# Turning the merged activations to channel-major with VectorE block transposes and DMAs through DRAM instead of TensorE transposes

## The chip, the cores and the metric

The kernel runs on one core of one Trainium2 chip. The metric is the device time of an execution in microseconds; a kernel's time is the median of its runs. A core has five engines with instruction streams of their own: TensorE (PE, matrix products), VectorE (DVE), ScalarE (ACT), GpSimd (POOL) and SyncE (SP, which here only issues DMAs). Each engine works through its stream in order, and engines wait for each other by semaphores.

## The reference

One layer of a decoder trunk on 256 tokens of 2048 channels. After an RMSNorm, one wide projection feeds three branches (stick-breaking attention, a Mamba-2 scan, cross-attention into 256 memory tokens) and three sets of gates. What matters here is the end:

```python
gates = sigmoid(gate_pre + b_gate)
g_sb, g_ssd, g_mem = split(gates, 3)
merged = (g_sb * (o_sb @ w_branch_sb)
          + g_ssd * (o_ssd @ w_branch_ssd)
          + g_mem * (o_mem @ w_branch_mem))
x = x + merged @ w_out
return rms_norm(x, final_norm_w)
```

All is float32. The kernel keeps the precision by splitting each operand of a product into a high and a low part and adding three products.

## The kernel before, in words

**Layout.** `merged` is held token-major: two tiles of 128 tokens x 2048 channels. The last product contracts over channels, so its left operand must be channel-major: `mT`, a `Cols` object of sixteen blocks of 128 channels (four to a slot), each with a high and a low half of 128 x 256 tokens. Turning `merged` into `mT` is the subject of the change.

**A gemm.** `gemm` (L249) computes 256 tokens x 512 output channels. It goes over the contraction in chunks of two 128-row blocks. For each chunk `load_chunk` (L205) issues a DMA of 512 KB of weights on SP's queue into a `raw` buffer (four of them, `RAWB`). `split` (L142) lets ScalarE write the high part `wh` (L146) and VectorE the low part `wl` (L150), each with three buffers. Then come twelve matmuls (L266 to L268): for each of two blocks and two token halves high x high, high x low, low x high. A gemm over 2048 rows has 16 blocks, eight chunks.

**The order of work.** The code is emitted by hand in program order and each engine keeps that order. After each chunk `pump` (L185) advances a counter, runs what has fallen due, and takes one step of other work from one of two lanes. `defer(fn, chunks)` (L172) puts `fn` on a heap, due so many chunks later. `gemm` defers its evacuation by `LATE` = 3 chunks, so it is emitted in the middle of the next gemm, behind that gemm's third chunk on every queue.

**The stage of the change.** The loop at L866 takes the branches in the order memory, stick-breaking, scan, and for each four groups `g` of 512 channels: a gate gemm (hidden state times gate weights, evacuated with bias and sigmoid into `sig`) and a branch gemm, whose `branch_evac` (L850) multiplies by the gate on VectorE (L857) and adds into `merged` on GpSimd (L858). For the third branch (`br == 2`), a group of `merged` is then complete. One chunk later `merged_cols` (L834) is emitted twice: TensorE turns eight 128x128 blocks into PSUM (L838), and two chunks after that `split` writes their high and low parts into `mT`. For `g` = 0 to 2 this falls into the gate gemm of the next group; for `g` = 3 into the first of the four output gemms. These read `mT` block by block, so that in their first gemm chunk 6 (blocks 12, 13) and chunk 7 (blocks 14, 15) need the last group.

**The output.** Three output gemms (L932) use `gemm`; the fourth (L936 on) splits its weights into slots first and computes the token halves one after the other, so that the first half is normalised and written while the second is computed.

The tiles of `slot` (L66) come from one pool of 16 buffers of 8 KB per partition.

Of the kernel before, what the change touches and what calls it, by code (L numbers as in the profile page):

```python
# [10 lines left out]
F32 = mybir.dt.float32  # L11
# [5 lines left out]
P = 128  # L17
D = 2048
T = 256
NKT = D // P  # L20
GW = 512
# [4 lines left out]
LATE = 3  # L26
# [15 lines left out]
def trunk_kernel(  # L42
# [6 lines left out]
    nc = tc.nc  # L49
# [6 lines left out]
    dram = ctx.enter_context(tc.tile_pool(name="dram", bufs=1, space=bass.MemoryType.DRAM))  # L56
# [5 lines left out]
    def nm(s):  # L62
        cnt[0] += 1
        return f"{s}_{cnt[0]}"

    def slot(shape, dt=F32, n="slot"):  # L66
        return big.tile(shape, dt, tag="slot", name=nm(n))

    def t4(shape, n="t4"):
        return tmp.tile(shape, F32, tag="t4", name=nm(n), bufs=2)  # L70
# [16 lines left out]
    def bank(shape, n="bank"):  # L87
        return psB.tile(shape, F32, tag="bank", name=nm(n))
# [11 lines left out]
    ident = const.tile([P, P], F32, name="ident")  # L100
# [41 lines left out]
    def split(*parts):  # L142


        for hi, _, src, scale in parts:
            nc.scalar.activation(hi, src, AF.Copy, **({} if scale is None else {"scale": scale}))  # L146
        for hi, lo, src, scale in parts:
            h32 = hi.bitcast(F32)
            if scale is None:
                nc.vector.tensor_tensor(lo, src, h32, ALU.subtract)  # L150
            else:
                nc.vector.scalar_tensor_tensor(lo, src, scale, h32, ALU.mult, ALU.subtract)
# [19 lines left out]
    def defer(fn, chunks=LATE):  # L172

        cnt[0] += 1
        heapq.heappush(late, (now[0] + chunks, cnt[0], fn))
# [9 lines left out]
    def pump():  # L185


        now[0] += 1
        while late and late[0][0] <= now[0]:
            heapq.heappop(late)[2]()  # L190
        advance(lanes[now[0] % 2])

    def finish():
        while lanes[0] or lanes[1]:
            for lane in lanes:
                advance(lane)
# [8 lines left out]
    def load_chunk(w, c0, width, k0, kc):  # L205
        raw = stage.tile([P, kc, width], F32, tag="raw", name=nm("raw"), bufs=RAWB)
        nc.sync.dma_start(
            raw, w[k0 * P:(k0 + kc) * P, c0:c0 + width].rearrange("(k p) n -> p k n", p=P))
        return raw
# [36 lines left out]
            nc.scalar.activation(dst, acc[:, :, 1], AF.Copy)  # L246
            nc.vector.tensor_tensor(dst, acc[:, :, 0], dst, ALU.add)

    def gemm(lhs, nk, w, c0, evac):  # L249

        acc2 = psA.tile([P, 2, GW], F32, tag="acc", name=nm("acc"), bufs=2)
        acc = [acc2[:, 0], acc2[:, 1]]
        kc = KC
        for k0 in range(0, nk, kc):
            raw = load_chunk(w, c0, GW, k0, kc)
            wh = stage.tile([P, kc, GW], F32R, tag="wh", name=nm("wh"))
            wl = stage.tile([P, kc, GW], F32R, tag="wl", name=nm("wl"))
            split((wh, wl, raw, None))
            for j in range(kc):
                kt = k0 + j  # L260
                lh, ll = lhs.at(kt)
                first, last = kt == 0, kt == nk - 1
                for t in range(2):
                    a = acc[t]
                    tt = slice(t * P, (t + 1) * P)
                    nc.tensor.matmul(a, lh[:, tt], wh[:, j], start=first, stop=False)  # L266
                    nc.tensor.matmul(a, lh[:, tt], wl[:, j], start=False, stop=False)  # L267
                    nc.tensor.matmul(a, ll[:, tt], wh[:, j], start=False, stop=last)  # L268
            pump()
        defer(lambda: evac(acc))  # L270

    def to_cols(dst, b0):

# [165 lines left out]
    for g in range(4):  # L439
        gemm_cols(memT, NKT, w_mem_kv, 2 * g * P, to_split_cols(kT, 2 * g),  # L440
                  acc=None if g else [bank([P, 2, T], "acc") for _ in range(2)])
# [161 lines left out]
    for g in range(2):  # L603
        gemm(hT, NKT, w_in, C_SBV + g * GW, to_rows(vS, g * GW))
# [226 lines left out]
    merged = [slot([P, D], F32, "merged") for _ in range(2)]  # L831
    mT = []

    def merged_cols(k0):  # L834
        ps = bank([P, 2, T], "mt")
        for j in range(2):
            for t in range(2):
                nc.tensor.transpose(ps[:, j, t * P:(t + 1) * P],  # L838
                                    merged[t][:, (k0 + j) * P:(k0 + j + 1) * P], ident)
        defer(lambda: split((*mT[0].at(k0, 2), ps, None)), 2)  # L840

    def gate_evac(c0, sig):
        nc.scalar.dma_start(sig[:, 0], b_gate[c0:c0 + GW].partition_broadcast(P))
        def evac(acc):
            for t in (1, 0):
                nc.vector.tensor_tensor(sig[:, t], acc[t], sig[:, 0], ALU.add)
            defer(lambda: sigmoid(sig), 1)
        return evac

    def branch_evac(br, g, sig):  # L850
        cs = slice(g * GW, (g + 1) * GW)
        def evac(acc):
            for t in range(2):
                if br == 0:
                    nc.vector.tensor_tensor(merged[t][:, cs], acc[t], sig[:, t], ALU.mult)
                else:
                    nc.vector.tensor_tensor(sig[:, t], acc[t], sig[:, t], ALU.mult)  # L857
                    nc.gpsimd.tensor_tensor(merged[t][:, cs], merged[t][:, cs], sig[:, t],  # L858
                                            ALU.add)
            if br == 2:  # L860
                for pr in range(2):
                    defer(lambda pr=pr: merged_cols(4 * g + 2 * pr), 1)
        return evac

    branches = ((4096, oM, 8, w_branch_mem), (0, oS, 8, w_branch_sb), (2048, None, 16, w_branch_ssd))
    for br, (g0, src, nk, wb) in enumerate(branches):  # L866
        for g in range(4):
            sig = t4([P, 2, GW], "sig")
            gemm(hT, NKT, w_in, C_GATE + g0 + g * GW, gate_evac(g0 + g * GW, sig))
            if src is None:  # L870
                finish()
                mT.append(Cols(NKT, "mT"))
                src = oD[0]
            gemm(src, nk, wb, g * GW, branch_evac(br, g, sig))


    yo = [slot([P, D], F32, "yo") for _ in range(2)]
# [58 lines left out]
    g = 3  # L936
# [9 lines left out]
    for t in range(2):  # L946
        tt = slice(t * P, (t + 1) * P)
        for cs in (slice(0, GW),) if t == 0 else (slice(0, T), slice(T, GW)):
            acc = psA.tile([P, 2, GW], F32, tag="acc", name=nm("acc"),
                           bufs=2)[:, 0, 0:cs.stop - cs.start]  # L950
# [50 lines left out]
```

## Time and profile before

| what | value |
|---|---|
| median of 3 runs | 1228.02 us (1227.74 to 1228.5) |
| span of the profiled execution, first to last instruction | 1226.6 us |
| TensorE busy | 1215.5 us |
| VectorE / ScalarE / GpSimd busy | 784.2 / 649.1 / 51.2 us |
| read from HBM / written | 239.48 MB / 2.13 MB |
| mean granted TensorE clock | 0.998 |

The profile is of one execution. Of that execution the profile gives the span only; the runs' median lies 1.4 us above it, which is what surrounds the first and the last instruction. A row of a timeline reads: start in us, duration in us, engine, source line, operation, written tile `<-` read tiles, shape, count, and in brackets how long the engine was idle before it and what ended the idling. A suffix q (SPq, ACTq) marks a DMA issue on that engine's queue: its duration is that of issuing, not of moving the data. In the chain of work that ended last a row is start, duration and what the time went to. A row for a tile or a line gives durations in ns as minimum/median/maximum. A row of windows gives the stretch and its length, the busy time of PE, its weight loads, VectorE, ScalarE and GpSimd, the granted clock, the DMA share and GB/s. A row of DMA issues ends with the KB of each and the median us from issue to landing.

### The profile page before, as it was taken

The page shows a single profiled execution, that of the slowest core. Times are in us where ns is not written, and L with a number is a line of the kernel's source. Part 1 is how long each engine was busy: PE and PEld are TensorE (multiplying, and loading weights), DVE is VectorE, ACT ScalarE, POOL GpSimd, SP SyncE. Part 2 cuts the span into 40 slices and gives each one's busy share as a digit, 9 for nine tenths or more (in the row PEclk, how much of TensorE's full clock was granted, in tenths as well). Part 3 has the DMA queues.
Part 4 walks back from the last instruction along what each step waited for, and adds up shares of the span by engine and source line. Part 5 has one row for each costly group of instructions (what it writes and reads, how often), then busy time and mean ns, then how long its engine had stood idle before and what let it go on. Part 6 is the DMA issues. An engine that isn't in the chain of part 4 may idle for free.

```text
span 1226.6 us, 16569 instructions
## 1 busy us (share of the span) xinstructions
PE 1215.5 (99%) x6388; PEld 1034.8 (84%) x6388; DVE 784.2 (64%) x990; ACT 649.1 (53%) x875; POOL 51.2 (4%) x50
## 2 busy tenths in 40 slices
PE   9999999999999999999999999999999999999997
PEld 7888888888888888888888888888888888888886
DVE  5686554565654555888888758676777755555554
ACT  6765443554445454545665756475756544444443
POOL 0000000000000000010100000000000010110101
PEclk9999999999999999999999999999999999999999
DMA  9966566655566656565567667686766666567673
GB/s 340 342 197 187 163 194 189 187 168 165 166 180 182 187 172 182 169 182 173 177 185 223 207 200 218 180 231 181 231 184 192 202 195 205 188 197 240 204 240 107
DMA packets 175023, 242.70 MB, mean 198 GB/s; under 512 B 10272, under 2 KB 109792, under 8 KB 174816
## 3 DMA queue, kind: packets, MB, share of 16 engines
q1 hardware_dynamic: 168224, 229.51, 61.2%
q10 hardware_dynamic: 6720, 12.13, 3.0%
q8 instruction: 50, 0.82, 0.3%
q14 instruction: 29, 0.24, 0.1%
HBM read 239.48 MB, written 2.13 MB: 197 GB/s over the span
## 4 chain that ended last, share of the span: by engine, by line
PE 96%; DMA 1%; issue 1%; DVE 1%; ACT 1%; SPq 0%; POOLq 0%; POOL 0%; ACTq 0%
PE acc L229 29%; PE acc L266 15%; PE acc L267 15%; PE acc L268 15%; PE acc L233 14%; PE acc L398 1%; PE acc L399 1%; PE acc L397 1%; PE y L773 1%; DMA raw<-in_w_out_dram 1%; DMA raw<-in_w_mem_kv_dram 1%; PE dtp L459 0%; PE xp L730 0%; PE mt L838 0%; PE spo L649 0%
## 5 line engine op out<-in xcount | busy, mean ns | idle before, releaser
L150 DVE TENSOR_TENSOR wl<-raw,wh 128x1024 fp32r<-128x1024 f32 (+1 forms) x409 | 502.8, 1233 | 310.3 <-ACT wh L146 308.1
L146 ACT ACTIVATE wh<-raw 128x1024 fp32r<-128x1024 f32 (+1 forms) x409 | 431.0, 1055 | 382.5 <-PE acc L268 200.7
L229 PE MATMUL acc<-hT,wh 128*128 128x512 f32 x1408 | 444.0, 397 | 0.0
L233 PEld LDWEIGHTS acc<-hT,wl 128*128 128x128 f32 x1408 | 264.5, 188 | 62.5
L233 PE MATMUL acc<-hT,wl 128*128 128x256 f32 x1408 | 276.8, 278 | 0.0
L229 PEld LDWEIGHTS acc<-hT,wh 128*128 128x128 f32 x1408 | 214.4, 189 | 0.1
L266 PE MATMUL acc<-wh,hT 128*128 128x512 f32 x448 | 175.9, 393 | 0.0
L267 PE MATMUL acc<-wl,hT 128*128 128x512 f32 x448 | 174.7, 390 | 0.0
L268 PE MATMUL acc<-wh,hT 128*128 128x512 f32 x448 | 174.6, 390 | 0.0
L266 PEld LDWEIGHTS acc<-wh,hT 128*128 128x128 f32 x448 | 84.1, 188 | 17.7 <-ACT sq L146 0.5
L268 PEld LDWEIGHTS acc<-wh,hT 128*128 128x128 f32 x448 | 84.1, 188 | 17.8
L267 PEld LDWEIGHTS acc<-wl,hT 128*128 128x128 f32 x448 | 84.1, 188 | 17.4 <-DVE wl L150 0.6
L266 PE MATMUL acc<-wh,oD 128*128 128x512 f32 x128 | 49.8, 389 | 0.0
L267 PE MATMUL acc<-wl,oD 128*128 128x512 f32 x128 | 49.8, 389 | 0.0
L268 PE MATMUL acc<-wh,oD 128*128 128x512 f32 x128 | 49.8, 389 | 0.0
L687 DVE SCALAR_TENSOR_TENSOR cT<-cu,wcols,cT 128x255 f32<-128x255 f32 (+2 forms) x96 | 46.4, 483 | 3.4
L858 POOL TENSOR_TENSOR merged<-merged,sig 128x512 f32<-128x512 f32 x16 | 25.1, 1588 | 521.9 <-DVE sig L857 521.9
L229 PE MATMUL acc<-memT,wh 128*128 128x512 f32 x128 | 40.5, 398 | 0.0
L266 PE MATMUL acc<-wh,mT 128*128 128x512 f32 x96 | 37.4, 390 | 0.0
L268 PE MATMUL acc<-wh,mT 128*128 128x512 f32 x96 | 37.4, 389 | 0.0
L267 PE MATMUL acc<-wl,mT 128*128 128x512 f32 x96 | 37.4, 389 | 0.0
L630 POOL TENSOR_TENSOR lm<-lm,sp 128x384 f32<-128x384 f32 x8 | 13.1, 1639 | 394.7 <-DVE sp L629 385.0
(250 smaller groups left out, 1301.4 us busy)
## 6 DMA issues: line engine op xcount, KB each, us to landing
raw<-in_w_in_dram SPq DMA_DIRECT2D x288, 512.0 KB, 3.8
raw<-in_w_branch_ssd_dram SPq DMA_DIRECT2D x32, 512.0 KB, 4.1
raw<-in_w_out_dram SPq DMA_DIRECT2D x32, 512.0 KB, 5.1
raw<-in_w_mem_kv_dram SPq DMA_DIRECT2D x31, 512.0 KB, 6.6
raw<-in_w_branch_mem_dram SPq DMA_DIRECT2D x16, 512.0 KB, 4.1
raw<-in_w_branch_sb_dram SPq DMA_DIRECT2D x16, 512.0 KB, 4.5
dec<-acT SPq DMA_DIRECT2D x24, 256.0 KB, 6.2
sig<-in_b_gate_dram ACTq DMA_DIRECT2D x12, 256.0 KB, 4.7
```

What stands on the lines that cost most here:

```text
L146: nc.scalar.activation(hi, src, AF.Copy, **({} if scale is None else {"scale": scale}))
L150: nc.vector.tensor_tensor(lo, src, h32, ALU.subtract)
L229: nc.tensor.matmul(halves[b], wh[:, kt - k0, b * P:(b + 1) * P], lhs.both(kt), start=first, stop=False, skip_group_check=True)
L233: nc.tensor.matmul(halves[b][:, 1], wl[:, kt - k0, b * P:(b + 1) * P], lhs.at(kt)[0], start=False, stop=last, skip_group_check=True)
L266: nc.tensor.matmul(a, lh[:, tt], wh[:, j], start=first, stop=False)
L267: nc.tensor.matmul(a, lh[:, tt], wl[:, j], start=False, stop=False)
L268: nc.tensor.matmul(a, ll[:, tt], wh[:, j], start=False, stop=last)
L397: nc.tensor.matmul(a, lh[:, tt], wh[:, g], start=first, stop=False)
L398: nc.tensor.matmul(a, lh[:, tt], wl[:, g], start=False, stop=False)
L630: nc.gpsimd.tensor_tensor(lm, lm, sp, ALU.subtract)
L687: nc.vector.scalar_tensor_tensor(a[:, s:T], u[:, 0:T - s], convw[:, 3 - s, i:i + 1], a[:, s:T], ALU.mult, ALU.add)
L858: nc.gpsimd.tensor_tensor(merged[t][:, cs], merged[t][:, cs], sig[:, t], ALU.add)
```

## The change

`merged_cols` and its TensorE transposes go. A new function `turn` takes their place. For a group, VectorE transposes the 32x32 blocks of 128 tokens x 512 channels within the partitions, once for each token half; one DMA on SP's queue writes the result (512 KB) to a DRAM tile `turned`; two chunks later four DMAs on SP's queue read it back, each to 32 partitions and in pieces of 512 B, so that a channel's 256 tokens come to lie in one partition. Then four `split`s of one block each write `mT`, two of them two chunks after the reads and two of them three chunks after. `gemm` gets an argument for its evacuation's delay; it is 1 instead of 3 for the last group of the third branch. `turn` uses a further slot per group.

```diff
-    def gemm(lhs, nk, w, c0, evac):
+    def gemm(lhs, nk, w, c0, evac, chunks=LATE):
...
-        defer(lambda: evac(acc))
+        defer(lambda: evac(acc), chunks)
...
-    def merged_cols(k0):
-        ps = bank([P, 2, T], "mt")
-        for j in range(2):
-            for t in range(2):
-                nc.tensor.transpose(ps[:, j, t * P:(t + 1) * P],
-                                    merged[t][:, (k0 + j) * P:(k0 + j + 1) * P], ident)
-        defer(lambda: split((*mT[0].at(k0, 2), ps, None)), 2)
+    turned = [dram.tile([2, P, 4, 4, 32], F32, name=f"turned{i}") for i in range(4)]
+
+    def turn(g):
+
+        pair = slot([P, 2, 1024], F32, "turn")
+        blocks = pair[:, 0].rearrange("p (t j k c) -> p t j k c", t=2, j=4, k=4)
+        cols = pair[:, 1].rearrange("p (i k c) -> p i k c", i=8, k=4)
+        for t in range(2):
+            nc.vector.transpose(blocks[:, t].rearrange("p j k c -> p k j c"),
+                                merged[t][:, g * GW:(g + 1) * GW]
+                                .rearrange("p (k j c) -> p k j c", k=4, j=4))
+        nc.sync.dma_start(turned[g].rearrange("t p j k c -> p t (j k c)"),
+                          blocks.rearrange("p t j k c -> p t (j k c)"))
+
+        def back():
+            for j in range(4):
+                nc.sync.dma_start(
+                    cols[32 * j:32 * j + 32].rearrange("r i k c -> r i (k c)"),
+                    turned[g][:, :, j].rearrange("t (i r) k c -> r (t i) (k c)", r=32))
+            for k in range(4):
+                defer(lambda k=k: split((*[a.rearrange("p (i c) -> p i c", c=32)
+                                           for a in mT[0].at(4 * g + k)],
+                                         cols[:, :, k], None)), 2 + k // 2)
+        defer(back, 2)
...
             if br == 2:
-                for pr in range(2):
-                    defer(lambda pr=pr: merged_cols(4 * g + 2 * pr), 1)
+                defer(lambda: turn(g), 1)
...
-            gemm(src, nk, wb, g * GW, branch_evac(br, g, sig))
+            gemm(src, nk, wb, g * GW, branch_evac(br, g, sig), 1 if br == 2 and g == 3 else LATE)
```

## The prediction

> **What bounds the kernel now.** I read the page first: the span, the engines' busy shares and the chain that ended last.
>
> ```profile
> span 1226.6 us, 16569 instructions
> ...
> PE 1215.5 (99%) x6388; PEld 1034.8 (84%) x6388; DVE 784.2 (64%) x990; ACT 649.1 (53%) x875; POOL 51.2 (4%) x50
> ...
> PE 96%; DMA 1%; issue 1%; DVE 1%; ACT 1%; SPq 0%; POOLq 0%; POOL 0%; ACTq 0%
> ```
>
> TensorE (PE) holds 96% of the chain. So an instruction taken from PE is worth its whole length, and work given to VectorE (DVE, 64% busy) costs nothing so long as PE is never made to wait. The question is what feeds PE, so next I read the waits of SP's queue, which issues every weight load.
>
> ```profile
> SPq L207 <- DVE wl L150: 817.6, 329, 5.7
> ```
>
> A load waits until VectorE has finished splitting the chunk that held its raw buffer, four chunks earlier, and SP issues in program order: what stands behind a waiting issue waits too. How early the loads go out is seen in the timeline where the third branch's first group ends and the next gate gemm begins (call its chunks 0, 1, 2 ...): PE, then SP, then ScalarE, VectorE and GpSimd.
>
> ```profile
> 994.95 0.39 PE L266 MATMUL acc<-wh,hT 128*128 128x512 f32 x1
> ```
> ```profile
> 986.62 3.09 SPq L207 DMA_DIRECT2D raw<-in_w_in_dram  x2
> 992.06 0.37 SPq L207 DMA_DIRECT2D raw<-in_w_in_dram  x1
> 994.78 0.37 SPq L207 DMA_DIRECT2D raw<-in_w_in_dram  x1
> ```
> ```profile
> 995.15 1.06 ACT L146 ACTIVATE wh<-raw 128x1024 fp32r<-128x1024 f32 x1 [1.66 <-PE acc L268]
> 997.87 1.06 ACT L146 ACTIVATE wh<-raw 128x1024 fp32r<-128x1024 f32 x1 [1.66 <-PE acc L268]
> 1000.59 1.06 ACT L146 ACTIVATE wh<-raw 128x1024 fp32r<-128x1024 f32 x1 [1.66 <-PE acc L268]
> ```
> ```profile
> 996.24 1.23 DVE L150 TENSOR_TENSOR wl<-raw,wh 128x1024 fp32r<-128x1024 f32 x1 [1.49 <-ACT wh L146]
> 997.39 1.28 DVE L857 TENSOR_TENSOR sig<-acc,sig 128x512 f32<-128x512 f32 x2
> 998.96 1.65 DVE L150 TENSOR_TENSOR wl<-raw,wh 128x1024 fp32r<-128x1024 f32 x1 [0.30 <-ACT wh L146]
> ```
> ```profile
> 998.24 3.53 POOL L858 TENSOR_TENSOR merged<-merged,sig 128x512 f32<-128x512 f32 x2 [40.82 <-DVE sig L857]
> ```
>
> PE starts chunk 0 at 994.95. The three ScalarE rows are the high parts of chunks 2, 3 and 4, one per 2.72 us: that is PE's time for a chunk. The multiply L857 is emitted after chunk 2, and indeed stands right behind chunk 2's low part (996.24). Loads 2 and 3 are the pair at 986.62, load 4 goes out at 992.06, load 5 at 994.78. Chunk 4 is due on PE at 994.95 + 4 x 2.72 = 1005.83, so load 4 leaves 13.8 us ahead.
>
> **What goes.** The 32 TensorE transposes, eight for each of the four groups of columns. The chain shows a group's eight:
>
> ```profile
> 1006.00 0.87 PE mt L838 x8
> 1050.42 0.87 PE mt L838 x8
> 1094.83 0.87 PE mt L838 x8
> 1139.24 0.87 PE mt L838 x8
> ```
>
> 0.87 us each time, so 0.109 us for one, and 3.5 us in all. Nothing hides them on PE; the whole 3.5 is gained. The Trainium skill prices this otherwise: "VectorE: DVE Perf Modes", section "The three transpose paths", gives 390 ns for a 128x128 bf16 transpose on TensorE against 311 on VectorE, and by it 32 of them would free 12.5 us and the forecast below would fall by 9. The rows here are of these very transposes in their pipelined place, so 0.109 decides.
>
> **Work that moves beside PE.** VectorE gets two block transposes of 128x512 a group. None is in the trace; nearest are element-wise passes.
>
> ```profile
> L855 DVE TENSOR_TENSOR merged<-acc,sig x8: 679/682/686, 703.0 to 813.1; 128x512 f32<-128x512 f32 x8
> ```
> ```profile
> L655 DVE TENSOR_TENSOR so<-spo,zS x8: 415/417/424, 438.4 to 621.1; 128x256 f32<-128x256 f32 x8
> L146 ACT ACTIVATE oS<-so x8: 417/418/420, 438.8 to 621.5; 128x256 fp32r<-128x256 f32 x8
> L150 DVE TENSOR_TENSOR oS<-so,oS x8: 424/425/426, 439.3 to 622.0; 128x256 fp32r<-128x256 f32 x8
> ```
>
> I take 0.68, the row of the same shape, with bounds of 0.42 (half the elements) and 1.23 (twice). The split becomes four pieces of 256 elements (ScalarE 4 x 0.42, VectorE 4 x 0.43) in place of two of 512: under 1 us more per group on engines that idle over 1 us per chunk, and the pieces are first used many chunks later, except in the last group. There the emission order puts pieces 0 and 1 just before chunk 6, which reads them, and the DMAs that bring them land some 3 us earlier by the times below. Cost: nothing.
>
> **The wait that is added.** Per group SP gets one write to DRAM and, two chunks later, four reads. The write is emitted after chunk 3, so in SP's order it stands **behind load 3 and ahead of load 4**, and it waits for the transposes, these for GpSimd's merged sums. The second sum ends at 998.24 + 3.53 = 1001.77, the second transpose 0.1 + 0.68 later: the write leaves at 1002.6. SP reached it at about 990, and load 4, due out at 992.06, is held until 1003.0 (0.37 for an issue): 11 us late. What follows needs a landing time.
>
> ```profile
> DMA to landing us min/median/max: 3.5/4.4/5.5
> ```
> ```profile
> GB/s 340 342 197 187 163 194 189 187 168 165 166 180 182 187 172 182 169 182 173 177 185 223 207 200 218 180 231 181 231 184 192 202 195 205 188 197 240 204 240 107
> ```
> ```profile
> dec<-acT SPq DMA_DIRECT2D x24, 256.0 KB, 6.2
> ...
> out_dram<-yo SPq DMA_DIRECT2D x4, 256.0 KB, 3.2
> ```
>
> The first row is the 512 KB raw loads of this stretch. The DMA engines will be empty but for the write's 512 KB just ahead, 1.5 us at the 340 GB/s of the first of the 40 slices. So load 4 takes 3.5 + 1.5 = 5.0 (bounds 3.5 and 7.0) and lands at 1008.0; high part 1.06, low part 1.23, small gaps: split at 1010.35. PE can do one matmul (0.23) without the low part, so it is due at 1006.06. **First stall: 4.3 us.** Load 5 follows load 4 closely enough to be covered.
>
> Then load 6 stands behind the four reads, and these wait for the write to land: 4.0 (3.2 for 256 KB plus 0.75 for the other half; upper bound 6.2) gives 1006.6. Four issues:
>
> ```profile
> L726 SPq DMA_DIRECT2D dec<-acT x24: 319/422/739, 660.2 to 870.1; - x24
> ```
>
> At 0.42 each, load 6 leaves at 1008.3, lands 5.0 later, is split at 1015.65; PE, resumed at 1010.35, wants it at 1015.8. That is a tie. It can only go one way, and the reads are pieces of 512 B of which no row here is a measure: I take 0.5 (bounds 0 and 2). Each group of the first three: 4.3 + 0.5 - 0.87 = +3.9, together **+11.8**. Sixteen chunks lie between two writes; a feed that runs at 4.4 + 1.06 + 1.23 us per four chunks wins back its lead in that time.
>
> **The last group** is emitted earlier: multiply after chunk 0 of the first output gemm, transposes and write after chunk 1, reads after chunk 3. PE starts that gemm's chunk 0 at 1128.20.
>
> ```profile
> 1128.20 0.39 PE L266 MATMUL acc<-wh,mT 128*128 128x512 f32 x1
> ```
> ```profile
> 1154.81 2.56 POOL L888 TENSOR_TENSOR yo<-yo,fw 128x512 f32<-128x512 f32 x2 [19.51 <-ACT junk L887]
> ```
>
> The multiply starts at 1128.4, the sums 0.85 later (as 997.39 to 998.24), and end at 1132.8 (1131.8 if they take 2.56 as in this row); the write leaves at 1133.6. Held behind it now is load **2**, which therefore leaves at 1134.0, lands at 1139.0 and is split at 1141.35, while PE is due at 1128.20 + 2 x 2.72 + 0.23 = 1133.87. Stall 7.5. VectorE's order also changes (chunk 1's low part waits behind the multiply until about 1131.3, just when PE wants it): nothing. One thing more hangs on a gap so long, the granted clock:
>
> ```profile
> 1218.26 0.28 PE L956 MATMUL acc<-wlh,mT 128*128 128x256 f32 x1
> ```
> ```profile
> 1221.00:1222.00 1.00, 0.00 (x0) 0.00 (x0) 0.67 (x2) 0.58 (x2) 0.00 (x0) 1.00 0.24 82
> 1222.00:1223.00 1.00, 0.00 (x0) 0.00 (x0) 0.00 (x0) 0.17 (x1) 0.00 (x0) 0.70 1.02 373
> 1223.00:1224.00 1.00, 0.00 (x0) 0.00 (x0) 0.00 (x0) 0.00 (x0) 0.00 (x0) 0.50 0.97 379
> ```
>
> After PE's last matmul (ended 1218.54) PEclk stays 1.00 to about 1222.4 and is 0.50 from there: it halves after 3.9 us of idling. A gap of 7.5 will meet that, one of 4.3 barely. How long PE then stays slow no row shows; between nothing and one chunk at half rate (2.72), I take 1.4, which also hides the second tie. Last group: 7.5 + 1.4 - 0.87 = **+8.0**.
>
> Sum: 1226.6 + 11.8 + 8.0 = 1246.4 of span. The median lies 1.4 above the profiled span (1228.0 to 1226.6), so the forecast is **1248**.
>
> **Rivals.**
>
> 1. *The clock falls in every stall.* Nothing else changes, but three more falls at 0 to 2.7 each, say 2.3, give 1255. Against it: 4.3 is close to the 3.9 seen at the end. For it: a stall need only be a little longer, and 3.9 is one sample. The Trainium skill, "TensorE: Matmul & The Clock Gate", section "Part 1: The HAM clock gate", states a free-running window of about 3.4 us, half clock after one idle window and full clock after one busy one; by it a 4.3 us gap falls about one time in four, and a fall costs some 1.7 us. The trace's 3.9 us agrees with the first half; no row shows the second.
>
> 2. *Cheap path.* Transposes of 0.42, landings of 3.5 with nothing ahead, no tie, no clock loss, sums of 2.56 in the last group: chunk 4 split at 1002.3 + 0.37 + 3.5 + 2.35 = 1008.5 and a stall of 2.5 in each of the first three groups (net 1.6), chunk 2 at 1138.5 and 4.65 in the last (net 3.8); 1228.0 + 8.6 = 1237.
>
> 3. *Other side: the loads' lead covers the write.* Load 4 may leave as late as 1006.06 - 2.35 - 4.4 = 999.3 without PE noticing. If SP's queue does not hold it back that long, the transposes' 3.5 us are pure gain: 1224.5. The point of decision is a write that leaves before 998.9. GpSimd's sums alone end at 1001.77, whatever the transposes cost, so this needs load 4 to stand ahead of the write in the queue, against the order that the code emits. Even break-even, a stall of 0.87, needs 999.8.
>
> 4. *Half covered*, the stalls just eating the 3.5: within 2.5 us of 1228.
>
> **Chances.** Forecast as worked out 0.67; rival 1, 0.14; rival 2 or still less down to 1231, 0.10; rival 4, 0.04; rival 3, 0.05. A measurement of this kernel tells 0.2% (2.5 us) from no change. Faster 0.05, same 0.04, slower 0.91. With the bounds the low end is rival 2's 1237, rounded to 1236. All upper bounds at once (transposes 1.23, landings 7.0, ties of 2, the clock each time) would give some 1268, which needs every one of them; I stop at 1262.
>
> **What would show it.** Right: PE idle of about 4 us in the third branch's next three gate gemms, ended by the split of chunk 4, with ScalarE waiting for the raw load, and 7 us in the first output gemm at chunk 2; SP's waits show a long wait of the write for the transpose, about 12 us, and a wait of the reads for the write. Wrong: raw loads issued at their old cadence beside the waiting write, or block transposes over 1.5 us (VectorE then holds up the low parts too), or PE's gaps elsewhere, at the pieces that chunk 6 reads.

## The result, and the profile after

The changed kernel takes 1257.50 us in the median of four runs (1257.24 to 1258.37) against 1228.08 of the kernel before: a ratio of 1.0241, 95% interval 1.0227 to 1.0256, or 29.4 us more. The forecast was 1248, the range 1236 to 1262.

The page of the changed kernel: span, engines, the granted clock in 40 slices, the chain that ended last.

```profile
span 1256.6 us, 16555 instructions
...
PE 1225.2 (97%) x6356; PEld 1038.6 (83%) x6356; DVE 789.6 (63%) x1006; ACT 649.9 (52%) x883; POOL 51.2 (4%) x50
...
PEclk9999999999999999999999999999999988989999
...
PE 91%; DMA 3%; DVE 2%; issue 1%; ACT 1%; POOL 1%; SPq 0%; POOLq 0%; ACTq 0%
```

TensorE is busy 9.7 us *longer* than before although 32 transposes are gone, and three slices near the end show a clock of 8 in place of 9: a first sign that its matmuls ran slowly there. The rest is idling. These are the waits of TensorE from 985 to 1175 us (engine, line, waited for: us in total, times, longest); the kernel before has none in its part of the same work.

```profile
PE acc L266 <- ACT wh L146: 16.9, 4, 5.9
PE acc L267 <- DVE wl L150: 2.5, 5, 0.8
```

Four waits for a high part and five for a low one, 19.4 us. They lie at chunk 4 of the next three gate gemms and, of the first output gemm, at chunk 2 and, with one short wait for a low part, at chunk 1. The waits of SP's queue name what stands at the front:

```profile
SPq L845 <- DVE turn L842: 54.4, 4, 16.0
...
SPq L850 <- DMA turned<-turn: 5.9, 4, 1.6
```

Four writes wait 54.4 us for the transposes. How that reaches TensorE is seen in the timelines of the first group; the whole stretch lies 0.2 us later than in the profile of before. SP:

```profile
986.82 3.09 SPq L207 DMA_DIRECT2D raw<-in_w_in_dram  x2
1002.74 0.37 SPq L845 DMA_DIRECT2D turned<-turn  x1
1003.20 1.33 SPq L207 DMA_DIRECT2D raw<-in_w_in_dram  x2
1006.19 1.82 SPq L850 DMA_DIRECT2D turn<-turned  x4
1008.11 0.91 SPq L207 DMA_DIRECT2D raw<-in_w_in_dram  x2
```

ScalarE, which writes the high parts of chunks 3, 4, 5 and 6:

```profile
998.07 1.06 ACT L146 ACTIVATE wh<-raw 128x1024 fp32r<-128x1024 f32 x1 [1.66 <-PE acc L268]
1008.79 1.06 ACT L146 ACTIVATE wh<-raw 128x1024 fp32r<-128x1024 f32 x1 [9.65 <-DMA raw<-in_w_in_dram]
1011.14 1.06 ACT L146 ACTIVATE wh<-raw 128x1024 fp32r<-128x1024 f32 x1 [1.30 <-DVE wl L150]
1015.24 1.06 ACT L146 ACTIVATE wh<-raw 128x1024 fp32r<-128x1024 f32 x1 [3.04 <-DMA raw<-in_w_in_dram]
```

TensorE, from the last matmul of chunk 3 on:

```profile
1005.81 0.39 PE L268 MATMUL acc<-wh,hT 128*128 128x512 f32 x1
1009.90 0.79 PE L266 MATMUL acc<-wh,hT 128*128 128x512 f32 x1 [3.70 <-ACT wh L146]
1011.16 0.79 PE L267 MATMUL acc<-wl,hT 128*128 128x512 f32 x1 [0.47 <-DVE wl L150]
1011.75 0.63 PE L268 MATMUL acc<-wh,hT 128*128 128x512 f32 x1
1012.17 0.63 PE L266 MATMUL acc<-wh,hT 128*128 128x512 f32 x1
```

Loads 2 and 3 go out at 986.82, nothing after them until the write at 1002.74; load 4 follows at 1003.20, lands and is taken up by ScalarE at 1008.79, 9.65 us after ScalarE was ready. TensorE's second matmul of chunk 4, due at 1006.27 (two steps of 0.23 behind 1005.81), starts at 1011.16: 4.9 us late. Then the steps are 0.43 us (1011.75 to 1012.17) in place of 0.23. The windows around it, and two in the last group, show why (after the five busy times: PEclk, DMA share, GB/s):

```profile
1009.00:1010.00 1.00, 0.10 (x1) 0.10 (x1) 0.12 (x1) 0.84 (x1) 0.00 (x0) 0.94 1.23 161
1010.00:1016.00 6.00, 5.53 (x12) 3.98 (x13) 2.33 (x2) 1.82 (x2) 0.00 (x0) 0.50 1.08 294
1016.00:1017.00 1.00, 1.00 (x4) 0.84 (x3) 0.67 (x1) 0.69 (x2) 0.00 (x0) 0.64 1.04 385
...
1160.00:1161.00 1.00, 0.08 (x1) 0.08 (x1) 0.10 (x1) 0.87 (x1) 0.00 (x0) 0.54 1.17 208
...
1166.00:1167.00 1.00, 1.00 (x4) 0.77 (x4) 0.00 (x0) 1.00 (x1) 0.00 (x0) 0.55 1.04 385
```

0.94 over a microsecond that is either full or half clock means a fall at 1009.9, 3.7 us after TensorE's last matmul ended; 0.64 means a return at 1016.7. Six microseconds hold 12 matmuls instead of 26.

### The profile page after: what moved, and what is told of

Its sections match the earlier page's. It is cut to its first block, busy times and chain, and to the rows that moved or that the text cites. A ratio compares the mean times of both kernels' runs of the same rounds, so it can differ in the third digit from the quotient of the medians.

```text
span 1256.6 us, 16555 instructions
## 1 busy us (share of the span) xinstructions
PE 1225.2 (97%) x6356; PEld 1038.6 (83%) x6356; DVE 789.6 (63%) x1006; ACT 649.9 (52%) x883; POOL 51.2 (4%) x50
## 4 chain that ended last, share of the span: by engine, by line
PE 91%; DMA 3%; DVE 2%; issue 1%; ACT 1%; POOL 1%; SPq 0%; POOLq 0%; ACTq 0%
PE acc L229 28%; PE acc L233 14%; PE acc L267 14%; PE acc L266 14%; PE acc L268 14%; DMA raw<-in_w_in_dram 1%; DMA raw<-in_w_out_dram 1%; PE acc L398 1%; PE acc L399 1%; PE acc L397 1%; PE y L773 1%; POOL merged L875 1%; ACT wh L146 1%; DVE wl L150 1%; DMA raw<-in_w_mem_kv_dram 1%
## 5 line engine op out<-in xcount | busy, mean ns | idle before, releaser
L266 PE MATMUL acc<-wh,hT 128*128 128x512 f32 x448 | 179.5, 401 | 11.0 <-ACT wh L146 11.0
L267 PE MATMUL acc<-wl,hT 128*128 128x512 f32 x448 | 178.5, 399 | 1.7 <-DVE wl L150 1.7
L268 PE MATMUL acc<-wh,hT 128*128 128x512 f32 x448 | 177.6, 396 | 0.0
L266 PEld LDWEIGHTS acc<-wh,hT 128*128 128x128 f32 x448 | 86.2, 192 | 30.7 <-ACT wh L146 12.2
L268 PEld LDWEIGHTS acc<-wh,hT 128*128 128x128 f32 x448 | 86.2, 193 | 18.3
L266 PE MATMUL acc<-wh,oD 128*128 128x512 f32 x128 | 49.8, 389 | 0.0
L266 PE MATMUL acc<-wh,mT 128*128 128x512 f32 x96 | 38.5, 401 | 5.9 <-ACT wh L146 5.9
```

## The experiments

Theory A: the loads wait behind the write in SP's queue, and TensorE's clock falls in the gaps. Theory B: the added work itself costs, the block transposes on VectorE or 1 MB more of DMA traffic per group, wherever it is put. Each time stands beside runs of the kernel before on the same chip; their medians lay between 1227.6 and 1228.6.

**The write later in the same queue.**

```diff
-        nc.sync.dma_start(turned[g]..., blocks...)
+        def write():
+            nc.sync.dma_start(turned[g]..., blocks...)
+            defer(back, 3 if g < 3 else 2)
...
-        defer(back, 2)
+        if g < 3:
+            defer(write, 5)
+        else:
+            write()
```

> All of the change's instructions on the same queue; for the first three groups the write is emitted five chunks later and the reads three chunks behind it, so that SP reaches the write when the transposes are done. The last group is as in the change. Theory A (the loads wait behind the write in SP's queue, and TensorE's clock falls in the gaps): a group's cost of about 6.6 us goes and its gain of 0.87 stays, so 1257.5 - 3 x 6.6 = 1237.7, less some 2.6 where the gain had been counted in already: 1235 to 1238, with TensorE gaps left only in the first output gemm. Theory B (the added work itself, 1 MB more DMA traffic per group and the block transposes, is what costs): 1250 or more.

Measured: 1235.72 us, ratio 1.0066 (1.0051 to 1.0081), 21.8 us below the change. SP around the first group's write (L846), and all that TensorE waits for in the last:

```profile
986.79 14.39 SPq L207 DMA_DIRECT2D raw<-in_w_in_dram  x6
1003.82 0.37 SPq L207 DMA_DIRECT2D raw<-in_w_branch_ssd_dram  x1
1004.24 0.46 SPq L846 DMA_DIRECT2D turned<-turn  x1
1005.83 5.81 SPq L207 DMA_DIRECT2D raw<-in_w_branch_ssd_dram  x3
1011.73 1.90 SPq L853 DMA_DIRECT2D turn<-turned  x4
```
```profile
1129.17 0.50 PE L267 MATMUL acc<-wl,mT 128*128 128x512 f32 x1 [0.38 <-DVE wl L150]
1138.18 0.80 PE L266 MATMUL acc<-wh,mT 128*128 128x512 f32 x1 [6.22 <-ACT wh L146]
1139.44 0.80 PE L267 MATMUL acc<-wl,mT 128*128 128x512 f32 x1 [0.46 <-DVE wl L150]
```

Six loads run without a break where the change had a hole of 13 us, and the write finds its data ready. The instructions and the queue are the change's; only the place differs. Theory B falls for three groups, and what is left is the last group's gap.

**No DMA at all.**

```diff
-        nc.sync.dma_start(turned[g]..., blocks...)
-            for j in range(4):
-                nc.sync.dma_start(cols[32 * j:32 * j + 32]..., turned[g][:, :, j]...)
-        cols = pair[:, 1].rearrange("p (i k c) -> p i k c", i=8, k=4)
+        cols = pair[:, 0].rearrange("p (i k c) -> p i k c", i=8, k=4)
```

> The write and the four reads are left out; the parts of mT are split from the block-transposed tile itself, so mT holds wrongly ordered numbers of the same amount. Block transposes, splits and the early evacuation of the last group stay. Theory A: no gap is left but a few tenths in the first output gemm, where VectorE's order changed: 1228.1 - 3.5 + 0.5 = 1225. Theory B with the transposes as the cost: 1240 or more; with the DMA traffic as the cost: also 1225 (the late write tells these apart).

Measured: 1226.27 us (1224.73 to 1227.30), ratio 0.9984 (0.9974 to 0.9993): 1.7 us below the kernel before, where 3 had been expected. In this run's profile the first output gemm starts at 1125.7 against 1128.2 before: the first three groups give 2.5 us, the worth of their 24 TensorE transposes, so there the block transposes cost nothing. The last group gives nothing: its three gemms take 65.6 us against 65.5. VectorE's new order makes two low parts late there, chunk 1's by 0.5 us behind the multiply and chunk 2's by 0.15 behind the block transposes, which is most of 0.87. With this placing the whole idea has some 2 us to give.

**GpSimd's queue.** `nc.sync` becomes `nc.gpsimd` in the five DMAs of `turn`.

> The write and the reads are issued by GpSimd, which has nothing else to do there but the two sums, instead of SP; all else as in the change. Theory A: the loads keep their lead, no gap in the first three groups; in the last group the reads have a deadline before chunk 6 and may come up to 2 us late: 1225 to 1228. Theory B: 1245 or more, since the same bytes move and the same transposes run.

Measured: 1243.30 us (1239.52 to 1247.99), 14 below the change but well above what theory A had expected. GpSimd and then ScalarE in the first group:

```profile
1003.73 0.91 POOL L845 DMA_DIRECT2D turned<-turn  x1 [1.06 <-DVE turn L842]
1008.38 2.33 POOL L850 DMA_DIRECT2D turn<-turned  x4 [3.74 <-DMA turned<-turn]
```
```profile
1009.65 1.06 ACT L146 ACTIVATE wh<-raw 128x1024 fp32r<-128x1024 f32 x1 [1.66 <-PE acc L268]
1017.08 0.73 ACT L146 ACTIVATE mT<-turn 128x256 fp32r<-128x256 f32 x2 [6.37 <-DMA turn<-turned]
1017.72 1.04 ACT L146 ACTIVATE wh<-raw 128x1024 fp32r<-128x1024 f32 x1
```

The loads now keep their lead, and ScalarE stands: the splits of `mT` are emitted two chunks after the reads, but the data come 13.4 us after the write went out, and the next weight split is queued behind them. It is the same mechanism on another queue. On SP the stall had itself moved these splits back: in the changed kernel the first of them starts at 1017.58 and waits for nothing.

**TensorE kept busy in the gap.**

```diff
+        busy = bank([P, P], "busy")
+        for _ in range(16 if g < 3 else 26):
+            nc.tensor.matmul(busy, ones, ones, start=True, stop=True)
```

> The change with useless TensorE matmuls put where the gap is (16 of 128x128 behind chunk 3 of the first three groups, 26 behind chunk 1 in the last), about as long as the gap, so that TensorE is not idle and its clock should not fall; loads, write and reads are untouched. Theory A with the clock as a cost of its own (about 2.5 us a group, partly needed anyway because load 6 comes late): 1250 to 1253, granted clock 1.00 behind the gaps. If the clock costs nothing of its own (the slow stretch only covers a later wait): 1257. If the useless matmuls are too many: above 1258.

Measured: 1251.06 us, 6.4 below the change, with more matmuls done. TensorE (the trace counts two rows for each of the 16), and a window to compare with the 0.50 above:

```profile
1005.82 3.73 PE L850 MATMUL busy<-ones 128*128 128x128 f32 x32
1010.77 0.50 PE L267 MATMUL acc<-wl,hT 128*128 128x512 f32 x1 [0.77 <-DVE wl L150]
1017.21 0.50 PE L267 MATMUL acc<-wl,hT 128*128 128x512 f32 x1 [0.68 <-DVE wl L150]
```
```profile
1010.00:1016.00 6.00, 5.24 (x24) 4.29 (x24) 2.01 (x3) 2.12 (x2) 0.00 (x0) 1.00 1.08 313
```

The load comes hardly earlier (the second matmul starts at 1010.77 for 1011.16, and 0.2 of that is that the whole stretch lies earlier), but the clock holds: 24 matmuls in the six microseconds that held 12. The row at 1017.21 is a second wait, at chunk 6, that the change does not have.

**The same without the four reads**, and **the change without the four reads** (clock left to fall): the four lines of the reads go, and `cols` views the transposed half of the slot, as in the run without DMAs.

> The run with useless matmuls in the gaps, now without the four reads (mT is split from the block-transposed tile itself, so it holds wrongly ordered numbers). With the clock kept up, the second wait, load 6 behind the reads, should be what is left over the first stall: about 1.1 us a group by the trace of that run (0.7 to 1.0 of idle before chunk 6's second matmul). Theory A: 1251 - 4 x 1.1 = 1247. If the reads hold nothing: 1251.

> The change without its four reads; mT is split from the block-transposed tile itself and holds wrongly ordered numbers. The write and its wait on SP's queue stay, and TensorE's clock is left to fall. Theory A as sharpened by the runs so far: the first wait and the clock make up all of the 29.5 us, and the second wait (load 6 behind the reads), worth some 0.7 to 1.1 us a group with the clock kept up, is hidden by the slow clock here: 1255.5 to 1257.5. If the reads add to the cost here too: 1250 to 1254.

Measured: 1248.26 us, 2.8 below the run with reads (2.0 between the two profiled executions), and 1256.99 us (1254.26 to 1259.09), not to be told from the change. So the reads do hold load 6, worth 0.5 to 0.7 us a group, where the clock is kept up. At half clock TensorE comes late enough not to notice: the trace of the change has no wait at chunk 6. The two times alone would not show that, as the runs without reads are spread over 4.8 us.

**ScalarE's queue.** `nc.sync` becomes `nc.scalar` in `turn`.

> The change with its write and reads issued on ScalarE's queue. If the cost goes with what stands behind the waiting issue: the high parts now wait instead of the loads. The write leaves at 1002.7, where ScalarE wants chunk 4's high part at 1000.6 and TensorE wants its low part at 1006.3, so the write costs nothing in the first three groups; the reads and the splits behind them hold ScalarE up to 4 us beyond its lead: 1 to 3 us a group; the last group up to 5: 1230 to 1238, less than on SP's queue. Theory B: 1250 or more.

Measured: 1237.00 us, ratio 1.0065 (1.0050 to 1.0079). ScalarE in the first group:

```profile
1002.71 0.38 ACTq L845 DMA_DIRECT2D turned<-turn  x1
1003.22 2.01 ACT L146 ACTIVATE wh<-raw 128x1024 fp32r<-128x1024 f32 x2 [4.12 <-DVE turn L842]
...
1015.47 0.72 ACT L146 ACTIVATE mT<-turn 128x256 fp32r<-128x256 f32 x2 [5.49 <-DMA turn<-turned]
```

The write leaves within 0.03 us of its time on SP. The wait, the bytes and the instructions are the change's; behind it stand splits instead of loads. Chunk 4's high part starts 2.5 us late, its low part is done at about 1005.5, and TensorE reads it at 1006.22, so this delay is not noticed. 20 us of the 29 are gone.

**Two versions without such a wait.** Both turn the last group on TensorE, evacuated as before. One has the late write on SP; the other has the DMAs on GpSimd at the change's places, with the splits four chunks later.

```diff
-                defer(lambda: turn(g), 1)
+                if g < 3:
+                    defer(lambda: turn(g), 1)
+                else:
+                    for pr in range(2):
+                        defer(lambda pr=pr: merged_cols(4 * g + 2 * pr), 1)
...
-                                         cols[:, :, k], None)), 2 + k // 2)
+                                         cols[:, :, k], None)), 6 + k // 2)   # GpSimd's version
```

> The late write of the earlier experiment for the first three groups; the last group is turned by TensorE, and evacuated, as in the kernel before. Theory A: no wait of any load is left, and three times 0.87 us of TensorE time are saved: 1228.0 - 2.6 = 1225.4, ratio 0.998. Theory B (three groups of added DMA traffic and block transposes cost something themselves): at or above 1228.

> GpSimd issues the write and the reads of the first three groups at the change's places; the splits of what was read come four chunks later than in the change, since in the run from GpSimd's queue the reads landed 13.3 us after the write's issue and ScalarE stood 6 to 9 us at the first split, with the next weight split behind it. The last group as in the kernel before. If that wait of ScalarE was the whole cost of GpSimd's queue: 1225.4. If descriptors written by GpSimd slow the loads too: 1228 to 1235.

Measured: 1225.49 us (eight runs) and 1225.60 us (ten runs), both ratios 0.9975 (0.9965 to 0.9985): some 3 us below the kernel before. In the first of them TensorE's busy time against the 1215.5 of the kernel before:

```profile
PE 1212.8 (99%) x6364; PEld 1032.6 (84%) x6364; DVE 788.6 (64%) x1002; ACT 649.7 (53%) x881; POOL 52.2 (4%) x50
```

2.7 us less, for 24 transposes of 0.109 (2.6). The second run also settles GpSimd's queue for the first three groups: with the later splits nothing of its cost is left there, so it was ScalarE's early wait and not the queue as such. For the last group it settles nothing, since TensorE turns it here; in the run from GpSimd's queue its three gemms took 73.0 us (65.5 before), and there too ScalarE waited for the reads.

## Why the prediction was right, point by point

The time divides cleanly at the first output gemm. The row of the matmuls L266 that read `mT` has the start of the first and of the last of them; here it is in the profiles of before, of the change, of the late write and of the late write without the last group:

```profile
L266 PE MATMUL acc<-wh,mT x96: 389/389/476, 1128.2 to 1193.7; 128*128 128x512 f32 x96
```
```profile
L266 PE MATMUL acc<-wh,mT x96: 387/389/796, 1148.7 to 1223.4; 128*128 128x512 f32 x96
```
```profile
L266 PE MATMUL acc<-wh,mT x96: 388/389/796, 1125.7 to 1200.3; 128*128 128x512 f32 x96
```
```profile
L266 PE MATMUL acc<-wh,mT x96: 389/389/479, 1126.2 to 1191.8; 128*128 128x512 f32 x96
```

| | first three groups: start of the output against before | last group: length of its three gemms | from there to the end of the span |
|---|---|---|---|
| before | | 65.5 us | 32.9 |
| the change | +20.5 | 74.7 | 33.2 |
| late write | -2.5 | 74.6 | 33.6 |
| late write, last group on TensorE | -2.0 | 65.6 | 31.7 |

With the 0.2 us by which the change's profile lies later from the start, the first three groups cost 20.3, or 6.8 each (forecast 3.9), the last 9.2 (forecast 8.0). The last column varies by up to 2 us without any order by what was edited (31.3 to 33.6 over all profiles); I count no part of the change in it.

- *The transposes' worth.* 0.109 us each, by the rows of the page: confirmed, 2.7 us of busy time for 24. The Trainium skill's 390 ns ("VectorE: DVE Perf Modes", "The three transpose paths") would have made it 9.4, an estimate from that figure.
- *Block transposes on VectorE* cost nothing, and one takes 0.71 us against 0.68 assumed. In the row of tile `turn`, ns as minimum/median/maximum:

```profile
L842 DVE STREAM_TRANSPOSE turn<-merged x8: 697/705/714, 1000.7 to 1153.3; 128x512 f32<-128x512 f32 x8
```

- *The write leaves at 1002.6, load 4 behind it.* It left at 1002.74 in a stretch that lies 0.2 later. This step carried the forecast, and the late write showed it: 21.8 us come back by moving the five DMAs of each of three groups in the same queue.
- *First stall 4.3 us.* Measured 4.9 in the first group (4.4 and 5.3 in the next two): load 4 took 5.6 us from issue to ScalarE's start, not 5.0.
- *"That is a tie ... I take 0.5".* The second wait, load 6 behind the reads. Load 6 took 7.1 us (1008.11 to 1015.24), so by itself it would have been a wait; in the change it costs nothing, since the slow clock covers it.
- *The step that failed: "A gap of 7.5 will meet that, one of 4.3 barely."* No clock loss was charged to the first three groups. The clock fell in all four gaps and stayed at half for 6.8 us each time: its mean is 0.77 over the 15 us around each of the first three gaps and 0.83 over the 20 us around the last. The 3.9 us seen at the kernel's end, on which the step rested, was no threshold: before the second fall TensorE had stood only 3.2 us, run one matmul and begun to wait again. From 1011.16 to 1016.80 thirteen steps took 5.64 us instead of 2.95: 2.7 lost in the first group. That was rival 1, given 0.14, and its 2.3 per fall was near; the measured 1257.5 lies nearer its 1255 than the forecast's 1248, and that the range holds it is owed to the range's width, not to the sum. With it: 4.9 + 2.7 - 0.87 = 6.7 for the first group, against the 6.8 of the table.
- *The last group +8.0.* 9.2 by the table, and the changed kernel's trace finds 9.1 of it: 0.54 for VectorE's order at chunk 1, which had been put at nothing (a wait of 0.38 for the low part is in the late write's row at 1129.17); 7.1 at chunk 2 (forecast 7.5); 2.3 for the clock (forecast 1.4); less 0.87.
- *The other side*, loads that keep their lead, did not come: on SP the loads stood behind the write. It came as soon as the write was put where its data are ready.

- *The upper end.* All upper bounds at once, with 2.7 for each of the four falls, add up to some 1272, not 1268; nothing rests on it.

So the mechanism, its place and its sign were right; the clock's part in it was sized wrongly. The forecast was 9.5 us short. By the table 8.5 of that lie in the first three groups, where the clock is most of it, and 1.2 in the last; the profiled execution was 0.9 us longer than the median. On balance the clock adds 6.4 us to the whole, the difference that a busy TensorE made.

## What to carry to other kernels

A DMA that must wait for a late producer must not stand in a queue ahead of prefetches: ask when the queue reaches it, which is as far ahead of the compute as the prefetch runs, and emit it so much later, or on a queue whose next items have slack. The consumer of a round trip through DRAM needs the same care: from GpSimd's queue 13 us lay between the write and the use of the data. And price a stall of TensorE not by its length alone: here one of some 4 us also cost 2.7 us of half clock.

## What the runs showed of the hardware

The clock fell 3.7 us (first group) and 5.1 us (last, 0.54 in the window at 1160: a fall at 1160.1 behind a matmul that ended at 1155.0) after TensorE's last matmul, as it had 3.9 us after it at the end of the kernel before. It was back only 6.8 us after the fall in both (0.64 in the window at 1016, and 0.55 in that at 1166). That is not fixed: in the profile of the change without the four reads the second fall lasted 3.4 us (PEclk 0.77 from 1061 to 1062, 0.50 to 1064, 0.52 to 1065, then 1.00), the other three 6.8. The Trainium skill ("TensorE: Matmul & The Clock Gate", "Part 1: The HAM clock gate") gives at least one busy window of about 3.4 us for the return; half clock lasted one or two of these here. By its window, as an estimate, a gap of 4.3 us would have met a fall one time in four; four of four fell, and the other three runs of the change have the same mean clock of 0.987.

The length of one gap does not decide it. In the run from GpSimd's queue a wait of 1.04 us and one of 0.76 close behind it were followed by a fall (PEclk 0.76 from 1020 to 1021, 0.50 to 1023); in the run from ScalarE's queue 1.71 and 0.76 were not (PEclk 1.00 from 1060 to 1065). What does decide it, no run here shows. Useless matmuls of the gap's length were enough to prevent it.

A half clock is not pure loss: it hid a second wait that appeared, at 0.5 to 0.7 us a group, as soon as the clock was kept up.
